# Decoder trunk layer: the first merge's token tiles in the places of three token combinations, and dilated queries turned on chip

## The chip, the cores and the metric

One core of a Trainium2 chip runs the whole kernel. The metric is device microseconds of one execution, as a median of several runs; lower is better. Everything is float32, and matmul operands are split into a high part and a low part (each a tile that the program calls fp32r), so that one product is three matmuls: high by high, high by low, low by high.

## The reference

One layer of a decoder trunk over 1024 tokens of width 1024, cut to what matters here:

```python
xn = _modulate(_rmsnorm(x, norm1), sh1, sc1)
z = xn @ w_in                       # au av bx bg q k v (768 each), 3 gates of 1024
out_a = _mixer_a(a_u, a_v, ...)     # chunked gMLP
out_b = _mixer_b(b_x, b_g, ...)     # RG-LRU recurrence
out_c = _mixer_c(c_q, c_k, c_v, rel_table)
gates = sigmoid(z_gate.reshape(bsz, s, 3, D_MODEL))
merged = gates[0]*(out_a @ p_a) + gates[1]*(out_b @ p_b) + gates[2]*(out_c @ p_c)
x = x + g1 * (merged @ w_out)
...
def _mixer_c(q, k, v, rel_table):   # 12 heads of 64
    for window, dil in ((128, 1), (512, 4), (2048, 16)):
        o, l = _dilated_attn(q * 64**-0.5, k, v, window, dil, rel_table)
    # the outputs weighted by softmax of the log-sums, then summed
```

## The kernel before, in words

**The projection stream.** `xn @ w_in` runs as units of seven steps (a Strassen-Winograd scheme): in each step twelve matmuls of 512 columns (line 295) multiply one combination of a weight pair's blocks (A11, A12, S1, S2, S3, A22, S4) by one combination of the tokens (B11, B21, T1, T2, T3, T4, B22). Each token combination lies split in eight tiles of a pool of its own, `xc1B11`, `xc1B21` and so on. So B11 is read in the first step of a unit only, B21 in the second, T1 in the third. After a step ACT or DVE moves a PSUM bank into the output tile `ot` (L161, L163, L165, L267, L269, L170, L172); of `ot` there are two buffers. A step S3 adds into the bank that the evacuation L165 of S2 reads, and S4 into the bank that L269 reads, which comes after L267. The units stand in a list (`Stream`), and its order is kept on all five engines; weights are prepared some steps ahead (L252, L254, L258). Its last nine units are three for queries, three for keys, and the gate units 18, 20 and 22. Gate units end with sigmoids (L677) and stores into `g_scr`.

**Queries and keys.** After a query or key unit `split_heads` makes from each half of `ot` the high part `h` (L924, ACT) and the low part in place (L927 or L929, DVE), and stores them to DRAM. Queries are stored twice, in token order and in an order in which a block of 128 tokens has its four residues modulo four in runs of 32; the second order is made by ACT (L933). `late`, side work that is fed in beside these units, forms modulation vectors from `w_ada` (POOL's DMAs, DVE, four small matmuls at each end).

**Attention and the first merges.** Once side work of the `hl` and `ad` pools has ended, a pool `hd` takes their place and head 0 is loaded (`load_head`, POOL's queue, and 16 small bias loads on SP). Then a second phase interleaves 12 heads with the merges of the branches, in an order written as planned times: head h starts at time h, and merge work (`filler`) is spread over F0 to F1. Only TensorE's order is fixed there; the other engines are ordered by the compiler's scheduler, which also lets work of this phase in among the last steps of the stream. `logits` forms seven banks for a head: four of dilation 1 (`cfg` 0) with 128 neighbouring columns of `qp` as weights, and three of dilation 4 (`cfg` 1: two with six matmuls, four of 128 and two of 256 columns, and one with four of 256) whose weights are every fourth column of `qn` and whose moving columns are every fourth of the keys. Two banks take turns. `merge` needs its branch's tokens split into tiles `oT` (lines 1117, 116, 117), the branch's weights (`p_a`, line 124, split by 116 and 117) and gates from `g_scr`. `oT` lies in pools `mrg0` and `mrg1`, which open when the stream's pools close, over the places of B11, B21 and T1. From SP's queue DMAs are issued in order; `raw` tiles have four buffers.

Of the kernel before, what the change touches and what calls it, by code (L numbers as in the profile page):

```python
# [20 lines left out]
P = 128  # L21
# [15 lines left out]
LEAD, DQ, TM, DP, DO = 0.55, 0.08, 1.05, 0.11, 0.18  # L37
FL, F0, F1 = -0.2, 0.1, 13.3
# [31 lines left out]
def trunk(ctx: ExitStack, tc: tile.TileContext, I: dict, out: bass.AP, dbg=None):  # L70
# [22 lines left out]
    def rows_scr(name, n):  # L93
# [3 lines left out]
    qk_scr = {n: [dram.tile(sh, F32, name=f"{n}{h}_scr") for h in range(NH)]  # L97
              for n, sh in (("q", [2, 2, HD, S]), ("k", [2, HD, S]))}
# [174 lines left out]
    def stream_ws(gb, tcomb, views, ot, post):  # L273
# [10 lines left out]
        for i, (wn, tn, bk) in enumerate(ORDER):  # L284
# [123 lines left out]
    xc = {n: x1.enter_context(tc.tile_pool(name=f"xc1{n}", bufs=1, side="right"))  # L408
          for n in ("B11", "B21", "T1", "B22", "T4", "T3")}
# [263 lines left out]
    def project(col, dst, f, j):  # L673

        def post(m0, m1):
            flat = [m.rearrange("p a b -> p (a b)") for m in (m0, m1)]
            res = [(1, lambda i=i: act.activation(flat[i], flat[i], f)) for i in (1, 0) if f]  # L677
            return res + [(2 if f else 1, lambda i=i: nc.scalar.dma_start(dst[j + i], flat[i])) for i in (1, 0)]
# [237 lines left out]
    def store_heads(name, ix, j, t):  # L916
        for i in range(2):
            nc.scalar.dma_start(qk_scr[name][2 * j + i][ix], t[HD * i:HD * i + HD, :])

    def split_heads(name, j, m, scale, hlp):  # L920

        mf = m.rearrange("p a b -> p (a b)")
        h = hlp().tile([P, S], F32R, tag="hl", bufs=3, name="hl")
        act.activation(h, mf, AF.Copy, scale=scale)  # L924
        yield
        if scale == 1.0:
            dve.tensor_tensor(mf.bitcast(F32R), mf, h.bitcast(F32), op=OP.subtract)  # L927
        else:
            dve.scalar_tensor_tensor(mf.bitcast(F32R), mf, scale, h.bitcast(F32), op0=OP.mult, op1=OP.subtract)  # L929
        for c, src in enumerate((h.bitcast(F32), mf)):  # L930
            if name == "q":
                dst = hlp().tile([P, S], F32, tag="hl", bufs=3, name="hlp")
                act.activation(dst.rearrange("p (t r i) -> p t r i", t=NT, r=4),  # L933
                               src.rearrange("p (t i r) -> p t r i", t=NT, r=4), AF.Copy)
                store_heads("q", (1, c), j, src)
                yield
                store_heads("q", (0, c), j, dst)
            else:
                yield
                store_heads("k", (c,), j, src)  # L940

    def project_heads(name, j, hlp):
        def post(m0, m1):
            def queue():
                for i, m in ((1, m1), (0, m0)):
                    side.append(split_heads(name, j + i, m, -0.125 if name == "q" else 1.0, hlp))

            return [(1, queue)]
# [3 lines left out]
    def late(ad):  # L952
# [15 lines left out]
        for i, (a, h, k) in enumerate(order):  # L968
# [7 lines left out]
            if k:  # L976
                yield
# [20 lines left out]
        for q in range(2):  # L998
            scale_cols(mod2, "norm2", q)

# [47 lines left out]
    gate_units(18, 20)  # L1048
# [8 lines left out]
    def load_head(h):  # L1057
        def tl():
            return heads["hd"].tile([P, 2, S], F32R, tag="qk", bufs=2, name="qk") if h % 2 == 0 else \
                wk.tile([P, 2, S], F32R, tag="ot", bufs=2, name="qk")  # L1060

        qq, kk = tl(), tl()
        nc.gpsimd.dma_start(qq, qk_scr["q"][h].rearrange("a c b s -> (c b) a s"))
        for i in range(2):
            nc.gpsimd.dma_start(kk[HD * i:HD * i + HD], qk_scr["k"][h].rearrange("c b s -> b c s"))
        qp, qn, kh, kl = qq[:, 0], qq[:, 1], kk[:, 0], kk[:, 1]
# [660 lines left out]
```

## Time and profile before

| | |
|---|---|
| median of 3 runs | 1984.4 us (1983.62 to 1989.04) |
| the profiled execution's own time | 1982.27 us |
| its span, first to last instruction | 1980.6 us |
| TensorE busy | 1874.4 us, 95% of the span |
| VectorE, ScalarE, GpSimd busy | 1287.9, 899.5 and 633.8 us |
| mean granted TensorE clock | 0.984 of full speed |

Rows below give microseconds from the span's start. PE is TensorE's matmuls, PEld its weight loads, DVE VectorE, ACT ScalarE, POOL GpSimd; a name with q behind it is that engine's issuing queue. A figure in brackets at a row's end is the idle time of the engine ahead of that row and who ended it. A timeline row with x6 merges six instructions, and its time reaches to the end of the last.

### The profile page before, as it was taken

The numbers are of one execution on the slowest core, as the hardware profiler recorded it, in microseconds if no ns is written. First come the engines' busy times: TensorE is split into PE (matmuls) and PEld (weight loads), VectorE is DVE, ScalarE is ACT, GpSimd is POOL, SyncE is SP. The second block draws the span as 40 slices with busy tenths as digits, with TensorE's granted clock in tenths as the row PEclk, the third lists the DMA queues.
The fourth block names the chain that finished last, engine by engine and source line by source line (L and its number), as shares of the span: only waits on it lengthen the run. The fifth ranks groups of instructions, "written<-read, shape, count | busy, mean of one in ns | idle before, by whom it ended". The sixth has DMA issues, their size and how long they took to land.

```text
span 1980.6 us, 26351 instructions
## 1 busy us (share of the span) xinstructions
PE 1874.4 (95%) x9119; PEld 1508.4 (76%) x9119; DVE 1287.9 (65%) x2259; ACT 899.5 (45%) x1644; POOL 633.8 (32%) x1067
## 2 busy tenths in 40 slices
PE   6899999999999899899899999999999999999996
PEld 5767898877767677677777777877787887877885
DVE  6766576666666675555555765569767666557786
ACT  5344556664335633534434533444433443344543
POOL 6310000003111111244555565456544444300002
PEclk9899999999999999899999999999999999999998
DMA  9232435435556888777677445413334333477674
GB/s 326 70 122 84 140 104 165 140 129 173 172 178 218 291 243 235 217 167 188 166 167 186 126 169 181 150 64 123 122 114 149 99 97 124 135 271 254 201 228 147
DMA packets 248118, 328.61 MB, mean 166 GB/s; under 512 B 16551, under 2 KB 167315, under 8 KB 247984
## 3 DMA queue, kind: packets, MB, share of 16 engines
q1 hardware_dynamic: 197664, 184.07, 31.4%
q10 hardware_dynamic: 33744, 87.18, 12.1%
q0 software_dynamic: 16576, 55.67, 10.1%
q8 instruction: 72, 1.18, 0.2%
q14 instruction: 62, 0.51, 0.1%
HBM read 238.64 MB, written 88.22 MB: 165 GB/s over the span
## 4 chain that ended last, share of the span: by engine, by line
PE 72%; DMA 9%; DVE 6%; issue 6%; POOL 3%; ACT 2%; SPq 1%; ACTq 0%; DVEq 0%; POOLq 0%
PE g L191 18%; PE g L295 18%; PE gp L1152 7%; PE g L334 6%; PE g L1615 6%; PE go L1407 4%; PE sl L1214 3%; DMA adaw<-in_w_ada_dram 2%; PE g L215 2%; PE tp L1258 1%; PE o L1287 1%; PE gp L1370 1%; PE m L788 1%; DMA res<-x_scr 1%; PE o L1290 1%
## 5 line engine op out<-in xcount | busy, mean ns | idle before, releaser
L295 PE MATMUL g<-xs,wh 128*128 128x512 f32 x1344 | 435.9, 405 | 31.1 <-ACT ot L165 21.7
L191 PE MATMUL g<-xs,wh 128*128 128x512 f32 x1176 | 367.6, 394 | 9.5 <-DVE up L168 2.7
L295 PEld LDWEIGHTS g<-xs,wh 128*128 128x128 f32 x1344 | 251.3, 190 | 107.8 <-ACT ot L165 32.1
L116 ACT ACTIVATE wh<-raw 128x512 fp32r<-128x512 f32 (+2 forms) x251 | 147.2, 601 | 274.2 <-issue 58.8
L191 PEld LDWEIGHTS g<-xs,wh 128*128 128x128 f32 x1176 | 220.3, 188 | 63.0 <-ACT xs L116 3.1
L295 PE MATMUL g<-xs,wl 128*128 128x512 f32 x672 | 267.9, 399 | 0.0
L191 PE MATMUL g<-xs,wl 128*128 128x512 f32 x588 | 230.4, 393 | 0.0
L117 DVE TENSOR_TENSOR wl<-raw,wh 128x512 fp32r<-128x512 f32 (+2 forms) x180 | 129.8, 727 | 84.2 <-ACT wh L116 84.0
L1152 PE MATMUL gp<-oT,wh 128*128 128x512 f32 x512 | 171.7, 415 | 4.4 <-ACT oT L116 1.9
L295 PEld LDWEIGHTS g<-xs,wl 128*128 128x128 f32 x672 | 127.8, 190 | 31.2
L117 POOL TENSOR_TENSOR wl<-st,wh 128x512 fp32r<-128x512 f32 x63 | 104.0, 1651 | 144.3 <-ACT wh L116 139.4
L117 POOL TENSOR_TENSOR wl<-raw,wh 128x512 fp32r<-128x512 f32 (+2 forms) x71 | 92.3, 1301 | 123.1 <-ACT wh L116 108.4
L254 ACT ACTIVATE wh<-st 128x512 fp32r<-128x512 f32 x120 | 75.2, 627 | 120.6 <-DVE st L252 120.4
L191 PEld LDWEIGHTS g<-xs,wl 128*128 128x128 f32 x588 | 110.5, 188 | 24.9
L334 PE MATMUL g<-wh,xs 128*128 128x256 f32 x672 | 124.8, 286 | 0.0
L116 ACT ACTIVATE wh<-st 128x512 fp32r<-128x512 f32 x95 | 59.3, 628 | 138.9 <-PE g L191 96.8
L1222 ACT ACTIVATE pm<-pm,stat 128x128 f32<-128x128 f32 (+1 forms) x192 | 89.0, 465 | 58.0 <-DVE stat L1219 57.9
L1152 PEld LDWEIGHTS gp<-oT,wh 128*128 128x128 f32 x512 | 89.8, 192 | 27.2 <-issue 7.7
L334 PEld LDWEIGHTS g<-wh,xs 128*128 128x128 f32 x672 | 103.7, 188 | 1.6 <-issue 1.0
L1615 PE MATMUL g<-wl,wh 128*128 128x512 f32 x264 | 103.5, 392 | 0.0
L1615 PE MATMUL g<-wh,wl 128*128 128x512 f32 x264 | 103.4, 392 | 0.0
L1152 PE MATMUL gp<-oT,wl 128*128 128x512 f32 x256 | 102.7, 401 | 0.0
(321 smaller groups left out, 3790.2 us busy)
## 6 DMA issues: line engine op xcount, KB each, us to landing
raw<-in_w_in_dram SPq DMA_DIRECT2D x66, 512.0 KB, 5.7
raw<-in_f_wdown_dram SPq DMA_DIRECT2D x77, 256.0 KB, 3.7
adaw<-in_w_ada_dram SPq DMA_DIRECT2D x48, 256.0 KB, 5.4
g_scr<-ot ACTq DMA_DIRECT2D x24, 512.0 KB, 5.2
adaw<-in_w_ada_dram POOLq DMA_DIRECT2D x48, 256.0 KB, 5.1
raw<-g_scr SPq DMA_DIRECT2D x24, 512.0 KB, 3.6
qk<-q_scr POOLq DMA_DIRECT2D x12, 1024.0 KB, 6.1
qk<-k_scr POOLq DMA_DIRECT2D x24, 512.0 KB, 9.6
```

Of the source, the lines that this page charges most:

```text
L116: act.activation(h, src, AF.Copy)
L117: l_eng.tensor_tensor(l, src, h.bitcast(F32), op=OP.subtract)
L191: pe.matmul(banks[bk], a[:, k, :], b, start=(fresh and j == 0), stop=(j == 11), skip_group_check=True)
L215: pe.matmul(banks[i, h], a[:, k, :], b, start=(fresh and j == 0), stop=(not fresh and j == 11), skip_group_check=True)
L254: act.activation(it["h"], bl[name], AF.Copy)
L295: pe.matmul(banks[bk], a[:, k, :], b, start=(fresh and j == 0), stop=(j == 11), skip_group_check=True)
L334: pe.matmul(banks[t2][bk][:, 256 * i:256 * i + 256], a[:, sl], b[:, k % 2, :], start=(fresh and i == 0 and j == 0), stop=(j == 11), skip_g ...
L1152: pe.matmul(pt, a_[:, k % g, :], b_, start=(j == 0), stop=(j == 3 * n - 1))
L1214: pe.matmul(sb[:, of:of + n], lq, kt[:, ks], start=(of == 0 and kt is kh), stop=(kt is kl), skip_group_check=True)
L1222: act.activation(pm[:, of:of + n], pm[:, of:of + n], AF.Exp, scale=-1.0, bias=stt[:, cfg, 0, idx:idx + 1], accum_out=stt[:, cfg, 1, idx:id ...
L1407: pe.matmul(pt, a_[:, sl], b_, start=(k == 0 and j == 0), stop=(k == KD - 1 and j == 2))
L1615: pe.matmul(bank, a_[:, sl], b_, start=(start and j == 0), stop=(j == 2), skip_group_check=True)
```

## The change

Three things. The tiles `oT` come from the pools of B11, B21 and T1 themselves, which now stay open for the merges, and the loads of branch a with the first gates and weights are written into the stream: first half of the tokens and gate 0 three steps from the end, second half and gate 1 two steps from it, the split of three tiles in the last step, the other nine behind it. The queries are stored once, high and low, in the four-residue order only; the copy is made by the split itself (ACT reads every fourth column), and the low part has a tile of its own, so that `ot` is not held by stores. For each head `turn_queries` makes from it on chip (two ACT copies of 512 columns) a tile `qd` in which the 128 queries of a residue, four tokens apart, lie side by side, so that the weights of the dilated logits are 128 neighbouring columns; keys are read as before. Also: both halves of a unit's output are finished each for itself (`post` takes one half), gate unit 20 moves behind the opening of `hd`, `late` yields six times in eight instead of seven, and heads are loaded 1.2 ahead instead of 0.55.

```diff
-LEAD, DQ, TM, DP, DO = 0.55, 0.08, 1.05, 0.11, 0.18
-FL, F0, F1 = -0.2, 0.1, 13.3
+LEAD, DQ, TM, DP, DO = 1.2, 0.08, 1.05, 0.11, 0.18
+F0, F1 = 0.1, 13.3
...
-                return later + (post(m0, m1) if wn == "S4" else [])
+                return later + (post(0, m0) if wn == "S4" else post(1, m1) if wn == "A22" else [])
...
+    mp_s = ctx.enter_context(ExitStack())
+    xc = {n: mp_s.enter_context(tc.tile_pool(name=f"xc1{n}", bufs=1, side="right")) for n in ("B11", "B21", "T1")}
...
+    def split_heads(name, j, m, hlp):
...
+        h, l = [hlp().tile([P, S], F32R, tag="hl", bufs=3, name="hl") for _ in range(2)]
+        if name == "q":
+            by4 = [t.rearrange("p (t r i) -> p t r i", t=NT, r=4) for t in (h, l)]
+            src = mf.rearrange("p (t i r) -> p t r i", t=NT, r=4)
+            act.activation(by4[0], src, AF.Copy, scale=-0.125)
+            yield
+            for r in range(4):
+                dve.scalar_tensor_tensor(by4[1][:, :, r, :], src[:, :, r, :], -0.125, by4[0][:, :, r, :].bitcast(F32),
+                                         op0=OP.mult, op1=OP.subtract)
...
-            if k:
+            if k % 4:
                 yield
...
+    def oT(h):
+        name = ("B11", "B21", "T1")[(12 * h + n_oT[h] % 12) // 8]
+        n_oT[h] += 1
+        return xc[name].tile([P, HALF], F32R, tag=name, bufs=8, name="oT")
...
-    gate_units(18, 20)
+    gate_units(18)
...
+    def turn_queries(qp):
+
+        qd = heads["hd"].tile([P, S], F32R, tag="qd", bufs=1, name="qd")
+        for j in range(0, S, HALF):
+            act.activation(qd[:, j:j + HALF].rearrange("p (r c i) -> p r c i", r=4, c=4),
+                           qp[:, j:j + HALF].bitcast(F32).rearrange("p (c r i) -> p r c i", r=4, c=4), AF.Copy)
+        return qd
...
-    gate_units(22)
+    gate_units(20, 22)
+    xa, first_a = {}, {}
...
+    for d, f in ((-3, lambda: xa.update(fetch_branch("a", 0, range(KW)))),
+                 (-3, lambda: first_a.update({0: fetch_merge("a", 0, 0)})),
+                 (-2, lambda: xa.update(fetch_branch("a", 1, range(KW)))),
+                 (-2, lambda: first_a.update({1: fetch_merge("a", 0, 1)})),
+                 (-1, lambda: split_some(0, (0, 1, 2)))):
+        marks.append((stream.n + d, f))
     stream.call(marks)
+    heads["qd"] = turn_queries(heads[0][0])
+    split_some(0, (3, 4, 5))
+    split_some(1, range(KW))
...
-                    lq = qn[:, 512 * j + r:512 * j + r + 509:4]
+                    lq = st_["qd"][:, P * idx:P * idx + P]
...
-        yield h - LEAD, load
+        yield max(h - LEAD, 0.3 * h), load
+        if h:
+            yield h - 0.3, turn_heads
```

On SP's queue, at the end of the stream, before the change: `raw` tiles (gates, and weights `p_a`) stand between the branch loads.

```order
L124 DMA raw<-g_scr 128x1024
L124 DMA raw<-in_p_a_dram 128x6x128
L1117 DMA oT<-oa_scr 128x512
L124 DMA raw<-g_scr 128x1024
L1117 DMA oT<-oa_scr 128x512
L124 DMA raw<-in_p_a_dram 128x6x128
L1117 DMA oT<-oa_scr 128x512 x3
L124 DMA raw<-g_scr 128x1024
L1117 DMA oT<-oa_scr 128x512 x6
L1172 DMA v_7105<-v_scr 128x8x128
```

And with it:

```order
L1098 DMA bt<-b_scr 32x256 x16
L1007 DMA oT<-oa_scr 128x512 x6
L124 DMA raw<-g_scr 128x1024
L124 DMA raw<-in_p_a_dram 128x6x128
L1007 DMA oT<-oa_scr 128x512 x6
L124 DMA raw<-g_scr 128x1024
L124 DMA raw<-in_p_a_dram 128x6x128
L124 DMA raw<-g_scr 128x1024
```

The bias loads have moved ahead of everything, each half of the branch comes in one run, and the first weights stand behind the first half.

On ACT, around the evacuations L165 and L267 of the stream's last unit, before (L677 are the last unit's sigmoids, L1222 the first head's exponentials):

```order
L678 DMA g_scr<-ot 128x1024 x2
L116 ACTIVATE wh<-raw 128x384 x4
L116 ACTIVATE oT<-oT 128x512
L165 ACTIVATE ot<-g 128x512
L116 ACTIVATE oT<-oT 128x512
L116 ACTIVATE wh<-raw 128x384
L116 ACTIVATE oT<-oT 128x512
L116 ACTIVATE wh<-raw 128x384
L267 ACTIVATE ot<-g 128x512
L1222 ACT_TABLE_LOAD
L1222 ACTIVATE pm,stat<-pm,stat 128x128
L1222 ACTIVATE pm,stat<-pm,stat 128x256 x3
```

And with it, from behind L267 on; ahead of these rows stand L165, one pair of weight splits (L116) and L267 (L678 are the sigmoids, L1256 the exponentials, L1105 the turned queries):

```order
L116 ACTIVATE oT<-oT 128x512 x3
L1256 ACT_TABLE_LOAD
L1256 ACTIVATE pm,stat<-pm,stat 128x128
L1256 ACTIVATE pm,stat<-pm,stat 128x256 x3
L678 ACT_TABLE_LOAD
L678 ACTIVATE ot<-ot 128x1024
L678 DMA g_scr<-ot 128x1024
L116 ACTIVATE wh<-raw 128x384 x2
L678 ACTIVATE ot<-ot 128x1024
L678 DMA g_scr<-ot 128x1024
L1105 ACTIVATE qd<-qp 128x512 x2
L116 ACTIVATE oT<-oT 128x512 x9
```

No split stands ahead of L165 any more, one pair of weights ahead of L267, and nine of the twelve token splits come behind both sigmoids and the turned queries.

On ACT in a query unit, before:

```order
L924 ACTIVATE hl<-ot 128x1024
L254 ACTIVATE wh<-raw 128x512
L933 ACTIVATE hlp<-hl 128x1024
L918 DMA q_scr<-hl 64x1024 x2
L254 ACTIVATE wh<-raw 128x512
L918 DMA q_scr<-hlp 64x1024 x2
L933 ACTIVATE hlp<-ot 128x1024
L918 DMA q_scr<-ot 64x1024 x2
L165 ACTIVATE ot<-g 128x512
```

And with it (L927 makes the high part, already in the four-residue order):

```order
L927 ACTIVATE hl<-ot 128x1024
L254 ACTIVATE wh<-raw 128x512
L918 DMA q_scr<-hl 64x1024 x2
L165 ACTIVATE ot<-g 128x512
L254 ACTIVATE wh<-st 128x512
L918 DMA q_scr<-hl 64x1024 x2
```

Both extra copies are gone from the place ahead of L165. On TensorE the matmuls are the same in number; the first eight of head 0's logits stood 36 matmuls ahead of the stream's end and now stand 120 ahead of it.

## Rows read from the trace of the kernel before

**Rows 1.** The page: its first line and TensorE's clock in 40 slices.
```profile
span 1980.6 us, 26351 instructions
PEclk9899999999999999899999999999999999999998
```

**Rows 2.** Windows: busy time and instructions of each engine, clock, DMA share and rate.
```profile
core 0: us, PE busy (x) PEld busy (x) DVE busy (x) ACT busy (x) POOL busy (x), PEclk, DMA share, GB/s
597.00:618.00 21.00, 20.31 (x86) 15.84 (x85) 12.96 (x22) 6.96 (x12) 3.75 (x7) 1.00 0.64 213
640.00:665.00 25.00, 21.91 (x87) 16.47 (x87) 15.96 (x24) 15.99 (x17) 3.30 (x7) 0.93 0.85 278
785.00:830.00 45.00, 33.78 (x131) 26.05 (x130) 19.11 (x55) 23.49 (x56) 11.08 (x38) 0.85 0.86 244
830.00:1176.00 346.00, 338.56 (x2032) 268.47 (x2031) 200.33 (x701) 150.17 (x484) 185.50 (x549) 0.99 0.65 159
```

**Rows 3.** Waits of TensorE from 785 to 830: total, times, longest.
```profile
PE g L295 <- DVE ot L269: 4.6, 1, 4.6
PE g L295 <- ACT ot L165: 2.2, 1, 2.2
```

**Rows 4.** Timeline at the end of the stream, ACT and TensorE.
```profile
786.48 0.94 ACT L116 ACTIVATE wh<-raw 128x384 fp32r<-128x384 f32 x2 [6.04 <-DMA raw<-in_p_a_dram]
...
787.84 0.57 ACT L165 ACTIVATE ot<-g 128x512 f32<-128x512 f32 x1
...
796.29 0.63 ACT L116 ACTIVATE oT<-oT 128x512 fp32r<-128x512 f32 x1 [2.88 <-DMA oT<-oa_scr]
...
797.24 0.58 ACT L267 ACTIVATE ot<-g 128x512 f32<-128x512 f32 x1
...
797.84 1.28 ACT L1222 ACT_TABLE_LOAD   x1
...
798.99 1.22 PE L295 MATMUL g<-xs,wh 128*128 128x512 f32 x2 [4.64 <-DVE ot L269]
...
799.54 0.49 ACT L1222 ACTIVATE pm<-pm,stat 128x256 f32<-128x256 f32 x1
```

**Rows 5.** Timeline in the query units, ACT and TensorE.
```profile
651.28 2.03 ACT L933 ACTIVATE hlp<-ot 128x1024 f32<-128x1024 f32 x1 [0.73 <-DVE adaa L975]
...
653.22 0.58 ACT L165 ACTIVATE ot<-g 128x512 f32<-128x512 f32 x1
...
653.85 1.22 PE L295 MATMUL g<-xs,wh 128*128 128x512 f32 x2 [3.08 <-ACT ot L165]
...
679.16 0.73 PE L295 MATMUL g<-xs,wh 128*128 128x512 f32 x2 [2.81 <-ACT ot L165]
```

**Rows 6.** ACT's copies of 128x1024: plain, and with every fourth column (ns min/median/max).
```profile
L924 ACT ACTIVATE hl<-ot x12: 1051/1056/1063, 621.6 to 745.7; 128x1024 fp32r<-128x1024 f32 x12
...
L933 ACT ACTIVATE hlp<-ot x6: 2028/2068/2096, 626.4 to 688.2; 128x1024 f32<-128x1024 f32 x6
```

**Rows 7.** Logits of one head, loads and matmuls: dilation 1 from 886.5, dilation 4 from 894.5.
```profile
L1214 PEld LDWEIGHTS sl<-qk x8: 187/189/192, 886.6 to 887.9; 128*128 128x128 f32 x8
...
L1214 PEld LDWEIGHTS sl<-qk x6: 315/330/333, 894.7 to 895.8; 128*128 128x128 f32 x6
...
886.85 0.62 PE L1214 MATMUL sl<-qk 128*128 128x128 f32 x4
887.31 0.49 PE L1258 MATMUL tp<-ident,pm 128*128 128x128 f32 x3
887.55 0.72 PE L1214 MATMUL sl<-qk 128*128 128x256 f32 x4
888.11 0.62 PE L1152 MATMUL gp<-oT,wh 128*128 128x512 f32 x2
...
894.92 1.55 PE L1214 MATMUL sl<-qk 128*128 128x128 f32 x6
896.40 0.66 PE L1287 MATMUL o<-st,v 128*64 128x128 f32 x8
...
901.07 1.32 PE L1214 MATMUL sl<-qk 128*128 128x256 f32 x4
902.21 0.62 PE L1258 MATMUL tp<-ident,pm 128*128 128x128 f32 x4
```

More of the change, by code (lines that the diff above doesn't have):

```diff
@@ L96, in trunk @@
     z_scr = {n: rows_scr(n, KW) for n in ("au", "bx", "bg")}
-    qk_scr = {n: [dram.tile(sh, F32, name=f"{n}{h}_scr") for h in range(NH)]
-              for n, sh in (("q", [2, 2, HD, S]), ("k", [2, HD, S]))}
+    qk_scr = {n: [dram.tile([2, HD, S], F32, name=f"{n}{h}_scr") for h in range(NH)]
+              for n in "qk"}
     g_scr = rows_scr("g", 3 * KD)
@@ L673, in project, with post @@
     def project(col, dst, f, j):
[L675 to L678, printed above, removed]
+        def post(i, m):
+            flat = m.rearrange("p a b -> p (a b)")
+            return [(1, lambda: act.activation(flat, flat, f)), (2, lambda: nc.scalar.dma_start(dst[j + i], flat))]
         return stream_ws(gb1, tcomb, pair_views(col, j), ot2, post)
@@ L942, in project_heads @@
-    def project_heads(name, j, hlp):
[L943 to L948, printed above, removed]
+        h, l = [hlp().tile([P, S], F32R, tag="hl", bufs=3, name="hl") for _ in range(2)]
[7 more added lines that the diff above has]
+                                         op0=OP.mult, op1=OP.subtract)
+        else:
+            act.activation(h, mf, AF.Copy)
+            yield
+            dve.tensor_tensor(l, mf, h.bitcast(F32), op=OP.subtract)
@@ L999, in late, with fetch_branch, split_branch, load_branch @@
             scale_cols(mod2, "norm2", q)
+    n_oT = [0, 0]
+    def oT(h):
+        name = ("B11", "B21", "T1")[(12 * h + n_oT[h] % 12) // 8]
+        n_oT[h] += 1
+        return xc[name].tile([P, HALF], F32R, tag=name, bufs=8, name="oT")
+    def fetch_branch(b, h, ks):
+        res = {}
+        for k in ks:
+            hh, ll = res[k, h] = oT(h), oT(h)
+            nc.sync.dma_start(ll.bitcast(F32), o_scr[b][k][:, HALF * h:HALF * h + HALF])
+        return res
+    def split_branch(b, tiles):
+        for (k, _), (hh, ll) in tiles.items():
+            split_to(hh, ll, ll.bitcast(F32), dve if b == "a" or k % 2 == 0 else pool)
+    def load_branch(b, h, ks):
+        res = fetch_branch(b, h, ks)
+        split_branch(b, res)
+        return res
+    def fetch_merge(b, zi, co, k0=0, k1=KW):
+        return (raw_tile(g_scr[zi * KD + co], [S]),
+                raw_tile(kview(I["p_" + b], co * P, P, k0 * P, k1 * P), [k1 - k0, P]))
     sched = ctx.enter_context(ExitStack())
@@ L1057, in load_head @@
     def load_head(h):
[L1058 to L1063, printed above, removed]
+        if h % 2 == 0:
+            qp = heads["hd"].tile([P, S], F32R, tag="qp", bufs=1, name="qp")
+            kk = heads["hd"].tile([P, 2, S], F32R, tag="qk", bufs=1, name="qk")
+        else:
+            qp, kk = [wk.tile([P, 2, S], F32R, tag="ot", bufs=2, name="qk") for _ in range(2)]
+            qp = qp[:, 0]
+        nc.gpsimd.dma_start(qp, qk_scr["q"][h].rearrange("c b s -> (c b) s"))
         for i in range(2):
             nc.gpsimd.dma_start(kk[HD * i:HD * i + HD], qk_scr["k"][h].rearrange("c b s -> b c s"))
-        qp, qn, kh, kl = qq[:, 0], qq[:, 1], kk[:, 0], kk[:, 1]
+        kh, kl = kk[:, 0], kk[:, 1]
         bt = heads["hd"].tile([P, 2, 256], F32, tag="bt", bufs=2, name="bt")
@@ L1326, in filler @@
     def filler():
-        xa, xb_, xc_ = {}, {}, {}
-        for h in range(2):
-            xa.update(load_branch("a", h, range(KW)))
-        yield
-        yield from merge("a", 0, emit_first, xa, lambda h: xb_.update(load_branch("b", h, range(KW))))
+        xb_, xc_ = {}, {}
+        yield from merge("a", 0, emit_first, xa, lambda h: xb_.update(load_branch("b", h, range(KW))), fetched=first_a)
         yield from merge("b", 1, emit_more, xb_, lambda h: xc_.update(load_branch("c", h, range(CSPLIT))))
```

58 lines of the change are left out of this document (17 added, 41 removed).

## The prediction, made before the changed kernel ran

> **What bounds the kernel now.** I read the page first: TensorE is granted nearly full speed everywhere, except in the first slice, one near the middle and the last [rows 1]. The slice near the middle is where the projection stream ends. Then the windows by stage [rows 2]. In a quiet unit (597 to 618) TensorE works 20.31 of 21 us; 86 matmuls are recorded, 0.236 us each, so a step of twelve takes 2.83 us. Three stretches differ. From 640 to 665 (query units) it idles 3.1 us and its clock is 0.93. From 785 to 830 (end of the stream, first merge, head 0) it works 33.78 of 45 us at a mean clock of 0.85. From 830 to 1176 (heads and merges) it works 338.56 of 346 us: there only fewer or shorter TensorE instructions help. No other engine comes near: DVE has 200.33 us, POOL 185.50, ACT 150.17 in that stretch.
>
> Next the waits of the end of the stream [rows 3]: TensorE stands still for 4.6 us until DVE's L269 and 2.2 until ACT's L165, both evacuations of the last unit; smaller waits make up the rest of the 11.2 us. The timeline says why [rows 4]. ACT's queue holds splits for the first merge ahead of the evacuations: it waits 6.04 us for the weights `p_a` with L165 behind, and 2.88 us for a token tile with L267 behind. L267 then starts at 797.24, L269 follows, and step S4 at 798.99. The weights and tokens come late because SP issues them in turn with `raw` tiles that wait for a buffer.
>
> In the query units the same evacuation L165 stands behind a 2.03 us copy with stride four, and TensorE waits 3.08 and 2.81 us for it [rows 5].
>
> **The end of the stream.** What it costs before: 11.2 us of idling, and the clock. At 0.85 over 45 us at most 6.75 us are lost to it, 5.1 if I count busy time alone (0.15 of 33.78). Together 16.3. In the changed order no split stands ahead of L165, so its wait falls to that of other units (about 0.7: the bank has to be moved before S3 may add to it). L267 has only one pair of weights ahead. I take the second wait as gone, and then add up what stands between L267 and the fourth token split, because TensorE needs that one for its ninth matmul of the first merge: L267 0.58, three token splits at 0.6, two table loads at 1.28, four exponentials at 0.49, two sigmoids of 128x1024 at 1.06 (priced as the plain copy), a pair of weights 0.94, two turned-query copies at 1.03 (half of 2.07 each), the split 0.6 [rows 4, 6]. That is 0.6 + 1.8 + 2.6 + 2.0 + 2.1 + 0.9 + 2.1 + 0.6 = 12.7 us after S3 ends. TensorE by then has done A22 and S4 (5.7), nine merge matmuls (2.1) and four logits (0.6): 8.4. So a **new wait of about 4.3 us** stands in front of the ninth merge matmul, with everything else of TensorE queued behind it, and a wait of 4.64 us was followed by slow matmuls (1.22 us for two, as against 0.73 elsewhere [rows 4, 5]); I add 2.5 us for that. With 0.7 for L165 and 1 us in case the first weights land late (they are now issued behind half the tokens, and the DMA engines are 0.86 busy [rows 2]): 8.5 us remain of 16.3. Gain 8. Bounds: 13 if the new wait doesn't cost, 2 if the weights are late by the old 6.04 us again.
>
> **The heads.** The weights of the dilated logits change from every fourth column to neighbouring columns. One load of the strided kind takes 330 ns, of the plain kind 189 [rows 7]. What matters is from start to start: a bank with four 128-column and two 256-column matmuls runs from 894.92 to 896.40, 1.48 us, and one with four of 256 from 901.07 to 902.21, 1.14. With plain weights and plain keys four of 256 took 0.56 (887.55 to 888.11), and two of 128 with two of 256 took 0.46, so 0.14 and 0.09 each. The keys remain strided, and no row has plain weights with strided keys. Bounds: if the keys cost nothing, the banks fall to 0.64, 0.64 and 0.56, which saves 2.26 us a head. If a 256-column matmul is held at 0.247 us (1.48 / 6) by its keys alone, and a 128-column one at half of that, the six take 0.99 and only the two mixed banks gain, 0.5 each: 1.0 a head. A mixed bank spends 0.247 per matmul though most have half the columns of the other bank, whose four take 0.285; so its short ones are surely held by the weights, the long ones perhaps by both. I take 1.2 a head, near the lower end because a moving column with stride four has no reason to be cheaper than a weight column with it. Eleven heads (head 0 lies in the stretch above): 13 us, bounds 11 and 25. If other engines swallow half, 5.5.
>
> For this ACT turns queries, 2.07 us a head [rows 6], 25 us in all, beside 150.17 busy of 346: its queue has room, and the copies stand 0.3 of a head ahead (a head takes 346 / 12, some 28 us, so 8 us) of the first logits that need them. Behind them in the queue are exponentials and the moves of turned probabilities, which TensorE needs later. DMA bytes fall (queries once instead of twice); nothing waits for them, I count nothing.
>
> The Trainium skill ("SBUF — State Buffer", the cacheline note in Door 1) says that SBUF is read in lines of 16 bytes and that every access to a new line pays. The trace agrees for ACT: 2068 ns against 1056 for the same elements [rows 6]. By that rule a stride of four float32 values pays in the keys as in the weights, the lower of my bounds.
>
> **The query and key units.** Per query tile ACT spent 1.06 + 2 x 2.07 us; now one strided copy, 2.07 [rows 6]. The copies ahead of L165 are gone and `ot` is free without its stores. DVE's low part becomes four strided pieces; DVE has room (15.96 of 25 us [rows 2]). The waits of 3.08 and 2.81 fall to 0.7 each (4.5), and the clock gives back at most 0.07 of 25 us (1.75 [rows 2]). Gain 5, bounds 6.2 and 0 (three `hl` tiles now serve four uses a unit and hold their places until stored; if ACT waits for them, L165 stands behind that).
>
> **Costed at nothing.** Finishing halves apart (three more table loads on ACT by the changed order, 3.8 us, hidden by TensorE's steps); `late` in fewer steps; head 0 loaded a unit earlier. This last has a price if its cover goes: head 0's first logits stand 120 matmuls from the end, 28 us (0.236 each); if the load is late, the whole stream waits behind them.
>
> **The sum.** 1982.3 us, the profiled execution's own time (1.7 more than its span, 2.1 less than the median of 1984.4), less 8, 13 and 5: **1956 us**.
>
> **Rivals.**
> - *Keys are free, weights were all.* 25 us in the heads instead of 13: 1944. For it: 330 ns loads in every dilated bank. Against: the keys have the same stride. The Trainium skill ("TensorE: Matmul & The Clock Gate", Back-to-back issue gap) says that spacing is set by load and matmul together, pipelined; no run here shows which of the two holds the long ones.
> - *The heads give little, or the new wait takes the end of the stream.* 5.5 in the heads, 4 at the end, 3 in the units: 1970. For it: DVE and POOL are over half busy in the heads, and a logits bank is free only when DVE has read it; a shorter bank then waits. Against: TensorE waits for little there (7.4 us in 346, [rows 2]).
> - *No change.* ACT's 25 us of copies and the 4.3 us wait eat the 26 us. That needs 2 us lost in each head; 1982.
> - *Slower.* One mechanism: TensorE waits in each head for ACT's two turned copies (2.07 us), with slow matmuls behind each wait as after the 3.08 us wait (1.22 for 0.73, some 1.5 us). 11 x 3.6 = 40 us against 26: 1996. It decides from 2.4 us a head. Against: 8 us between copy and use.
>
> **How the numbers follow.** Chances: the forecast (1948 to 1965) 0.5; free keys 0.15; little 0.21; no change 0.07; slower 0.07. Range: the ends of the bounds give 1982.3 - 13 - 25 - 6 = 1938 and 1982.3 - 2 - 5.5 = 1975; leaving out the last two cases, and the corners where all bounds meet, 1942 to 1972. A measurement here tells a change from none at about 0.3%, 6 us: faster (below 1978) 0.86, within 0.07, slower 0.07.
>
> **What would show it.** Right: no TensorE wait for L269 over 1 us at the end of the stream, one wait of 3 to 6 us for a token split (`oT`) in the first merge; L1248's loads at 189 ns throughout, mixed banks near 1.0 us from start to start, the four of 256 near 1.0 still; no waits over 1 us for L165 in the query units. Wrong: mixed banks at 0.64 (free keys); waits for `stat` or ACT's moves in each head; TensorE waiting for head 0's queries or bias ahead of the last unit.

## The result, and the profile after

The changed kernel takes 1964.6 us in the median (1961.2 to 1967.9), the kernel before 1984.9 beside it: ratio 0.9893, interval 0.9867 to 0.992. The first profiled execution of the changed kernel ran at a clock of 0.653 and took 2606.8 us, so the profile below is of a second profiled execution, the first experiment's: 1965.5 us with a span of 1963.4.

The page, its first line and the clock in slices:

```profile
span 1963.4 us, 26382 instructions
PEclk9899999999999999899999999999999999999998
```

The slice near the middle still falls below 9. To see where the time went, cut both executions at the same TensorE rows of the timeline: first row of the first query unit, of gate unit 18, of the last unit, the stream's last row, the 73rd merge matmul (the end of merge's first four banks), the last merge matmul.

| us | before | after | |
|---|---|---|---|
| up to the first query unit | 596.7 | 597.7 | +1.0 |
| six query and key units | 135.2 | 132.9 | -2.3 |
| gate units 18 and 20 | 42.1 | 42.6 | +0.5 |
| last unit | 30.1 | 20.6 | -9.5 |
| stream's end to the 73rd merge matmul | 34.9 | 39.9 | +5.0 |
| heads and merges, to the last merge matmul | 337.1 | 322.4 | -14.7 |
| the rest | 804.5 | 807.2 | +2.7 |

The last three stages ahead of the rest as windows, before (three rows) and after (last unit, up to the 73rd matmul, heads); columns as in [rows 2]:

```profile
774.00:804.10 30.10, 23.27 (x93) 18.13 (x91) 11.86 (x23) 15.21 (x29) 4.20 (x4) 0.89 0.80 242
804.10:839.00 34.90, 30.22 (x136) 24.24 (x136) 20.65 (x74) 17.07 (x51) 12.02 (x48) 0.90 0.82 202
839.00:1176.10 337.10, 329.94 (x1982) 261.04 (x1982) 192.10 (x666) 145.75 (x469) 181.92 (x535) 0.99 0.65 161
```

```profile
773.30:793.90 20.60, 19.91 (x85) 15.52 (x83) 8.83 (x20) 10.39 (x21) 1.59 (x2) 1.00 0.95 330
793.90:833.80 39.90, 29.34 (x137) 23.60 (x137) 22.75 (x77) 23.99 (x65) 16.15 (x51) 0.87 0.75 179
833.80:1156.20 322.40, 317.52 (x1981) 245.29 (x1980) 193.68 (x666) 155.27 (x488) 181.10 (x534) 0.99 0.61 152
```

In the last unit TensorE idles 0.7 us instead of 6.8, at full clock. The stretch behind it became worse: TensorE idles 10.6 us of 39.9 where it idled 4.7 of 34.9, and its clock is 0.87 for 0.90. In the heads, busy time fell by 12.4 us and idling by 2.3.

What TensorE waited for from 780 to 834, after (total, times, longest):

```profile
PE o L1321 <- POOL wl L117: 6.4, 1, 6.4
PE gp L1181 <- ACT oT L116: 3.0, 1, 3.0
PE gp L1181 <- DVE ot L172: 0.9, 1, 0.9
PE g L295 <- ACT ot L165: 0.7, 1, 0.7
```

The 4.6 us for L269 of [rows 3] are gone and L165 is at 0.7, as forecast. The forecast wait for a token split is there (3.0). The longest wait, 6.4 us, was in no forecast. The timeline shows both, put in order of time across the engines:

```profile
799.03 1.15 ACT L1105 ACTIVATE qd<-qp 128x512 fp32r<-128x512 f32 x2 [0.46 <-ACT ot L678]
...
800.75 1.52 PE L1181 MATMUL gp<-oT,wh 128*128 128x512 f32 x2 [3.02 <-ACT oT L116]
...
811.53 10.28 SPq L1098 DMA_DIRECT2D bt<-b_scr  x8
...
822.08 0.39 SPq L124 DMA_DIRECT2D raw<-in_p_a_dram  x1
...
825.53 0.94 ACT L116 ACTIVATE wh<-raw 128x384 fp32r<-128x384 f32 x2 [9.24 <-DMA raw<-in_p_a_dram]
...
826.09 0.56 DVE L117 TENSOR_TENSOR wl<-raw,wh 128x384 fp32r<-128x384 f32 x1 [4.75 <-ACT wh L116]
...
827.77 0.55 DVE L1297 COPY st<-tp 128x384 f32<-128x384 f32 x1
...
828.42 1.12 PE L1321 MATMUL o<-st,v 128*64 128x128 f32 x6 [6.43 <-POOL wl L117]
```

Read it upward. TensorE's first outputs need the turned probabilities `st`, which DVE copies at 827.77. Ahead of this copy in DVE's queue stands the low part of the fourth merge weights, which waits 4.75 us for ACT's high part, which waits 9.24 us for the load; SP issued the load at 822.08, behind eight bias loads that took it 10.28 us. (The row of waits names POOL's half of the same low part; it is DVE's that stands in the way.) The Trainium skill ("TensorE: Matmul & The Clock Gate", Architectural detail) says that VectorE and ScalarE take instructions strictly first in, first out. The trace agrees: the transposes that the copy reads had ended by 822.0, and 4.75 us of idle DVE stood ahead of it.

In the query units:

```profile
631.32 2.20 DVE L930 SCALAR_TENSOR_TENSOR hl<-ot,hl 128x256 fp32r<-128x256 f32 x4 [4.41 <-DMA q_scr<-hl]
...
638.27 0.69 DVE L269 TENSOR_TENSOR ot<-g,ot 128x512 f32<-128x512 f32 x1
...
639.01 0.73 PE L295 MATMUL g<-xs,wh 128*128 128x512 f32 x2 [2.44 <-DVE ot L269]
```

ACT no longer holds L165 up as in [rows 5], but DVE's low part waits for an `hl` tile that a store still reads, and DVE's L269, late behind it, holds TensorE up.

The dilated logits of one head, answering to [rows 7]:

```profile
887.84 1.10 PE L1248 MATMUL sl<-qk,qd 128*128 128x128 f32 x6
888.87 0.66 PE L1321 MATMUL o<-st,v 128*64 128x128 f32 x8
...
892.97 1.18 PE L1248 MATMUL sl<-qk,qd 128*128 128x256 f32 x4
893.97 0.62 PE L1292 MATMUL tp<-ident,pm 128*128 128x128 f32 x4
```

From start to start a mixed bank takes 1.03 us and the bank of four 256-column matmuls 1.00, where 1.48 and 1.14 were shown before.

### The profile page after: what moved, and what is told of

Read it like the earlier page. It is cut to its first block, busy times and chain, and to the rows that moved or that the text cites. A ratio compares the mean times of both kernels' runs of the same rounds, so it can differ in the third digit from the quotient of the medians.

```text
span 2604.6 us, 26382 instructions
## 1 busy us (share of the span) xinstructions
PE 2553.7 (98%) x9119; PEld 1689.1 (65%) x9119; DVE 1292.2 (50%) x2277; ACT 901.5 (35%) x1659; POOL 620.9 (24%) x1067
## 4 chain that ended last, share of the span: by engine, by line
PE 96%; issue 1%; DVE 1%; POOL 1%; ACT 1%; DMA 0%; POOLq 0%; DVEq 0%; SPq 0%
PE g L295 25%; PE g L191 22%; PE g L1647 10%; PE gp L1181 10%; PE g L334 6%; PE go L1439 5%; PE g L215 5%; PE sl L1248 3%; PE tp L1292 2%; PE o L1321 1%; PE o L1324 1%; PE gp L1402 1%; PE m L788 1%; PE m L884 1%; ACT ot L165 0%
## 5 line engine op out<-in xcount | busy, mean ns | idle before, releaser
L295 PE MATMUL g<-xs,wh 128*128 128x512 f32 x1344 | 568.3, 512 | 16.1 <-ACT ot L165 14.3
L191 PE MATMUL g<-xs,wh 128*128 128x512 f32 x1176 | 490.2, 507 | 0.0
L295 PEld LDWEIGHTS g<-xs,wh 128*128 128x128 f32 x1344 | 277.0, 209 | 189.1 <-issue 58.2
L295 PE MATMUL g<-xs,wl 128*128 128x512 f32 x672 | 341.7, 508 | 0.0
L191 PEld LDWEIGHTS g<-xs,wh 128*128 128x128 f32 x1176 | 243.3, 207 | 141.7 <-issue 47.4
L116 ACT ACTIVATE wh<-raw 128x512 fp32r<-128x512 f32 (+2 forms) x251 | 146.8, 600 | 478.7 <-PE g L191 143.4
L191 PE MATMUL g<-xs,wl 128*128 128x512 f32 x588 | 297.7, 507 | 0.0
L1181 PE MATMUL gp<-oT,wh 128*128 128x512 f32 x512 | 219.1, 518 | 1.0 <-DVE ot L172 0.9
L334 PE MATMUL g<-wh,xs 128*128 128x256 f32 x672 | 167.9, 349 | 0.0
L334 PEld LDWEIGHTS g<-wh,xs 128*128 128x128 f32 x672 | 139.3, 249 | 3.0 <-issue 1.9
L116 ACT ACTIVATE wh<-st 128x512 fp32r<-128x512 f32 x95 | 59.7, 629 | 231.8 <-PE g L191 211.1
L1647 PE MATMUL g<-wh,wl 128*128 128x512 f32 x264 | 133.8, 507 | 0.0
L1647 PE MATMUL g<-wl,wh 128*128 128x512 f32 x264 | 133.7, 507 | 0.0
L1181 PE MATMUL gp<-oT,wl 128*128 128x512 f32 x256 | 130.1, 508 | 0.0
L1647 PE MATMUL g<-wh 128*128 128x512 f32 x264 | 122.7, 507 | 0.0
```

The source lines that it names most:

```text
L116: act.activation(h, src, AF.Copy)
L191: pe.matmul(banks[bk], a[:, k, :], b, start=(fresh and j == 0), stop=(j == 11), skip_group_check=True)
L295: pe.matmul(banks[bk], a[:, k, :], b, start=(fresh and j == 0), stop=(j == 11), skip_group_check=True)
L334: pe.matmul(banks[t2][bk][:, 256 * i:256 * i + 256], a[:, sl], b[:, k % 2, :], start=(fresh and i == 0 and j == 0), stop=(j == 11), skip_g ...
L1181: pe.matmul(pt, a_[:, k % g, :], b_, start=(j == 0), stop=(j == 3 * n - 1))
L1647: pe.matmul(bank, a_[:, sl], b_, start=(start and j == 0), stop=(j == 2), skip_group_check=True)
```

## The experiments

Twelve runs. Each ratio is to the kernel before, run beside it, with its 95% interval; from one experiment to another it is ratios that are compared, and stages are read from one profiled execution each.

**The changed kernel again** (no edit).

> The changed kernel once more, for a profile with TensorE at full clock. It should take 1961 to 1968 us. The prediction's three terms are read from it: 8 us at the end of the stream, 13 in the heads, 5 in the query and key units. My theory before looking: since the total fell by 20 and not 26, the heads gave the lower bound or less (11 us), and the end of the stream 4 to 6, because the new wait for the fourth token split is there. Rival: the heads gave 13 or more and the query units nothing.

1965.4 us, ratio 0.989 (0.9869 to 0.9911). It is the base below. The theory of the heads fell (14.7 us, not 11 or less); that of the end of the stream held (4.5).

**Keys plain.**

```diff
-                    ks = slice(r, r + 4 * n - 3, 4)
+                    ks = slice(0, n)
```

> Keys of the dilated logits are read as neighbouring columns instead of every fourth (other keys, so other numbers come out; the instructions are the same). If strided keys hold the long matmuls of the dilated banks, the mixed bank falls to about 0.64 us and the bank of four 256-column matmuls to 0.56, and the time falls by a further 8 to 13 us. If the keys are free (the rival that would have given 1944), nothing changes, and the mixed bank is at 0.64 already.

1960.4 us, ratio 0.9854 (0.983 to 0.9878). Heads 316.9 us, 5.5 less than after the change and short of the 8 to 13 expected. The banks, in the timeline:

```profile
890.28 0.84 PE L1248 MATMUL sl<-qk,qd 128*128 128x128 f32 x6
891.05 0.66 PE L1321 MATMUL o<-st,v 128*64 128x128 f32 x8
...
894.89 0.74 PE L1248 MATMUL sl<-qk,qd 128*128 128x256 f32 x4
895.47 0.60 PE L1292 MATMUL tp<-ident,pm 128*128 128x128 f32 x4
```

0.77 and 0.58 us, against 1.03 and 1.00: the keys' stride costs what the change left in these banks. Over 22 mixed banks and 11 others that is 22 x 0.26 + 11 x 0.42 = 10.3 us, of which 5.5 reach the stage: shorter banks meet other waits, and TensorE idles 8.6 us there where it idled 4.9.

**Weights strided again, out of the turned tile.**

```diff
-                    lq = st_["qd"][:, P * idx:P * idx + P]
+                    lq = st_["qd"][:, HALF * j + r:HALF * j + r + 509:4]
```

> The turned tile is made but the dilated logits read every fourth column of it as weights, as the kernel before did (other queries, so other numbers come out). This undoes the heads' part alone and leaves ACT's turned copies. By the prediction's lower bound it costs 11 us against the changed kernel, by its value 13, and loads are at 330 ns again. If the heads gave little (the third rival), it costs 0 to 5 us.

1977.9 us, ratio 0.9951 (0.9933 to 0.9969); heads 335.2 us. The weight loads of one group of the lines (ns min/median/max) are those of before again:

```profile
L1248 PEld LDWEIGHTS sl<-qk,qd x165: 307/330/337, 839.8 to 1132.7; 128*128 128x128 f32 x165
```

So 335.2 - 322.4 = 12.8 us of the heads' 14.7 come from the weights alone.

**All first splits ahead of the turned queries.**

```diff
-                 (-1, lambda: split_some(0, (0, 1, 2)))):
+                 (-1, lambda: split_some(0, range(KW)))):
...
-    heads["qd"] = turn_queries(heads[0][0])
-    split_some(0, (3, 4, 5))
     split_some(1, range(KW))
+    heads["qd"] = turn_queries(heads[0][0])
```

> All six token splits of the first half stand in the stream's last step, and the second half's splits ahead of the turned queries. By the prediction the wait of about 4 us ahead of the first merge's ninth matmul then goes, with the slow matmuls behind it: 4 to 7 us less than the changed kernel. If that wait is not there, or another takes its place (the first dilated logits for the turned queries, S4 for L269), 0 to 2 us.

1963.3 us, ratio 0.9874 (0.9851 to 0.9896), which doesn't part it from the base. The profile shows that the 3.0 us wait is gone (2.3 for L172 and 2.1 for ACT's turned queries stand in its place), and the 6.4 us wait too, though the same weights are as late. In DVE's timeline the two instructions have changed places:

```profile
821.95 0.55 DVE L1296 COPY st<-tp 128x384 f32<-128x384 f32 x1
...
824.66 0.56 DVE L117 TENSOR_TENSOR wl<-raw,wh 128x384 fp32r<-128x384 f32 x1 [1.02 <-ACT wh L116]
```

So what late weights cost TensorE hangs on what the scheduler put behind their split: here it is no longer this copy.

**Branch loaded late.** The marks with the early loads are taken out, and the filler loads the branch itself again, in a first step at -0.2.

```diff
-    for d, f in ((-3, lambda: xa.update(fetch_branch("a", 0, range(KW)))),
...
-    split_some(0, (3, 4, 5))
-    split_some(1, range(KW))
...
+        for h in range(2):
+            xa.update(load_branch("a", h, range(KW)))
+        yield
+        yield from merge("a", 0, emit_first, xa, lambda h: xb_.update(load_branch("b", h, range(KW))))
```

> The changed kernel, with the loads and splits of the first branch and of the first two merges' weights put back behind the stream's end, as in the kernel before; their tiles stay where the change put them. Theory (early loading is worth the 8 us that the prediction gave the end of the stream): about 8 us slower than the changed kernel, 1973 us, with TensorE waiting over 10 us in all for the branch tiles between the last unit and the ninth merge matmul. Rival (most of it is given back anyway by a wait of 6 us some 25 us later, which the changed kernel has and this one has not): 2 to 4 us slower, 1968 us, and no wait of 6 us of the first outputs.

1962.5 us, ratio 0.9885 (0.9865 to 0.9906): not slower at all, where theory and rival both had a loss. Without them the last unit takes 23.7 us and the next stretch 34.6, together 58.3 against the base's 60.5 and 65.0 before. (These stages are of an execution of 1955.7 us, 6.7 below the run's median and its quickest.)

**The old places as well.** The former run, and the pools of the kernel before for the branch.

```diff
-        return xc[name].tile([P, HALF], F32R, tag=name, bufs=8, name="oT")
+        return mrg[h].tile([P, HALF], F32R, tag="oT", bufs=2 * KW, name="oT")
...
+    mp_s = ctx.enter_context(ExitStack())
+    mrg = [mp_s.enter_context(tc.tile_pool(name=f"mrg{h}", bufs=1, side="right")) for h in range(2)]
```

> The run with the branch loaded late, and its tiles put back as well where the kernel before had them, in pools of their own that open when the token combinations are closed; heads and query units stay changed. Theory (the places are what the end of the stream gains by, since the loads can start while the last unit runs; the explicit early loads add nothing): 8 to 11 us slower than with late loads alone, 1972 us, with branch loads still issued after the last unit's end and waits of several us for the branch and for L269 back in the last unit. Rival (the gain there comes from head 0 loaded a unit earlier and the smoother evacuation): within 3 us of late loads alone, 1963 us.

1953.7 us (1952.9 to 1956.7), ratio 0.9835 (0.9819 to 0.9852): the fastest version, clear of the changed kernel's interval. Undoing what the title names first, the places, with the early loads, gains some 11 us (0.0055 of 1985; the two intervals leave 6 to 16). The theory fell, and its rival was too timid. The windows of the same three stages:

```profile
772.70:794.50 21.80, 20.01 (x85) 15.52 (x83) 13.53 (x27) 15.17 (x31) 2.60 (x3) 1.00 0.89 302
794.50:827.80 33.30, 26.35 (x137) 22.17 (x137) 18.07 (x71) 18.24 (x51) 13.55 (x50) 0.98 0.78 179
827.80:1145.80 318.00, 315.76 (x1982) 243.96 (x1982) 194.23 (x666) 156.34 (x491) 181.75 (x534) 1.00 0.61 155
```

And TensorE's waits from 760 to 835, with one row of ACT's twelve splits of the branch:

```profile
PE sl L1236 <- ACT st L1283: 4.9, 1, 4.9
PE gp L1169 <- DVE ot L172: 2.0, 1, 2.0
PE g L295 <- ACT ot L165: 1.8, 1, 1.8
...
L116 ACT ACTIVATE oT<-oT x12: 614/618/634, 782.9 to 797.3; 128x512 fp32r<-128x512 f32 x12
```

The last unit is quick (21.8 us) without new places and without early loads, no wait for a token split is left, and the clock behind the stream is 0.98 where the base has 0.87. The fourth weights are late here too, at 4.9 us.

What then mended the last unit? SP's queue, before (four rows) and in this run (three rows):

```profile
767.78 10.21 SPq L1075 DMA_DIRECT2D bt<-b_scr  x11
...
778.62 0.39 SPq L124 DMA_DIRECT2D raw<-in_p_a_dram  x1
...
788.51 0.38 SPq L124 DMA_DIRECT2D raw<-in_p_a_dram  x1
...
798.53 0.32 SPq L124 DMA_DIRECT2D raw<-g_scr  x1
```

```profile
748.67 11.27 SPq L1095 DMA_DIRECT2D bt<-b_scr  x14
...
775.49 0.39 SPq L124 DMA_DIRECT2D raw<-in_p_a_dram  x1
...
778.53 7.20 SPq L1004 DMA_DIRECT2D oT<-oa_scr  x12
```

In the kernel before, the bias loads of heads 0 and 1 (eight each) held SP up to 778. Behind them came the second weights, and then branch loads cut up by `raw` tiles that waited for a buffer, among them the third weights at 788.51 and the fourth gate at 798.53; the last branch load started at 812.5. With the heads opened one unit earlier, fourteen of the sixteen bias loads are through at 759.9, 18 us sooner. Little of that reaches the loads behind: the second weights wait for a `raw` buffer and go out 3.1 us earlier, the first branch load 1.2 us earlier. The larger difference is that no `raw` tile stands between the twelve branch loads any more. They follow each other from 778.5, inside the last unit and not behind it as the theory had them, and ACT has seven of them split by the time it comes to L267. What is left of the change at this place is the earlier heads, the outputs finished half by half, gate unit 20 in a new place and `late` in fewer steps. These weren't run apart, so which of them put the loads into this order isn't shown.

**Bias loads later.**

```diff
+        def bias():
+            st_["in"] = st_["in"][:3] + (load_bias(h),)
...
+            yield h - 0.3, bias
             yield h - 0.3, turn_heads
```

> The changed kernel, with the bias loads of heads 1 to 11 moved from 1.2 heads to 0.3 heads ahead of their head, so that three of the eight that stood ahead of the fourth merge weights on SP's queue stand behind them. Theory (the wait of 6.4 us of the first outputs comes from the last of these bias loads, which waits for a queue slot held by a gate load): the weights are issued some 5 us earlier, the wait falls under 2 us, 1960 us. Rival (the weights are late because the transfers are slow there, whatever stands ahead of them on the queue): the wait stays at 4 us or more, 1965 us.

1968.1 us, ratio 0.9909 (0.989 to 0.9929): no gain. The weights' load, ACT's split and the outputs:

```profile
813.56 0.39 SPq L124 DMA_DIRECT2D raw<-in_p_a_dram  x1
...
822.53 0.94 ACT L116 ACTIVATE wh<-raw 128x384 fp32r<-128x384 f32 x2 [6.53 <-DMA raw<-in_p_a_dram]
...
825.87 0.33 PE L1327 MATMUL o<-st,v 128*64 128x128 f32 x2 [3.89 <-issue]
```

Issued 8.5 us earlier, the weights take 9.0 us to reach ACT where the base's took 3.5, and TensorE still waits 3.9 us. The place on the queue was a part of it; in the base the DMA share is above 1 from 805 to 820, so crowded transfers are the likely rest, which no run shows apart. The rival was nearer.

**High parts stored first.**

```diff
             act.activation(by4[0], src, AF.Copy, scale=-0.125)
+            store_heads(name, 0, j, h.bitcast(F32))
             yield
```

(the same for keys, and the call behind the low part is dropped)

> The changed kernel, with the stores of the high parts in the query and key units issued right behind ScalarE's copy instead of behind VectorE's low part. Theory (VectorE waits for a tile whose store is late, and its addition and TensorE behind it): the waits of the low part for a store fall from 16.6 us in all to under 9, TensorE's waits for L269 in the query units from 3.8 us to under 2, 1 to 3 us faster, 1963 us. Rival (the stores take so long that 1.3 us matter little, or VectorE's four slow pieces themselves make it late): within 1 us, 1965 us.

1961.2 us, ratio 0.9872 (0.9852 to 0.9891); the intervals overlap with the base. One wait of DVE (from 610 to 790) and one of TensorE (from 610 to 760):

```profile
DVE hl L931 <- DMA q_scr<-hl: 2.4, 1, 2.4
...
PE g L295 <- DVE ot L269: 1.4, 3, 0.8
```

The low part's waits fall from 16.6 us to 2.4, TensorE's for L269 from 2.6 to 1.4 (the 3.8 of the expectation counts one ahead of these units), and the query and key units from 132.9 us to 130.7. Part of DVE's waiting moved: for the weight blocks of the side work it waits 12.4 us instead of 4.0. The theory holds for the mechanism; its size is 2 us.

**Four tiles.** `hl` gets four buffers, `adaw` one instead of three, and a weight block of the side work is fetched only behind the use of the one before.

```diff
-        h, l = [hlp().tile([P, S], F32R, tag="hl", bufs=3, name="hl") for _ in range(2)]
+        h, l = [hlp().tile([P, S], F32R, tag="hl", bufs=4, name="hl") for _ in range(2)]
...
-                raws[i] = ad.tile([P, HALF], F32, tag="adaw", bufs=3, name="adaw")
+                raws[i] = ad.tile([P, HALF], F32, tag="adaw", bufs=1, name="adaw")
```

> The changed kernel, with four tiles for the high and low parts of queries and keys instead of three, paid for by one buffer instead of three for the weight blocks of the side work (which is loaded one block ahead). Theory (three tiles for four uses a unit are what the query units lack): no wait of the low part for a store over 1 us, no TensorE wait for L269 over 1 us in the query units, 2 to 4 us faster, 1962 us. Rival (VectorE's four pieces of 0.6 us and ScalarE's 2.1 us copy are what is late): TensorE's waits as before, 1965 us. If VectorE waits for the one buffer of the side work instead: the same or up to 3 us slower.

2048.0 us, ratio 1.0317 (1.0296 to 1.0338). Nothing follows for `hl`: the price swallowed the test. One wait of DVE and two of TensorE, from 590 to 900:

```profile
DVE adaa L967 <- DMA adaw<-in_w_ada_dram: 106.6, 42, 6.9
```

```profile
PE m L988 <- DVE adaa L967: 37.0, 4, 9.9
PE g L295 <- DVE ot L269: 24.0, 7, 7.5
```

With one buffer DVE waits 42 times for a weight block of the side work, and the evacuations stand behind it. The expectation's 3 us for this case was too low by far.

**Plain query split.** High and low parts are written in the order read, one DVE instruction of 1.2 us for four; other queries reach the heads.

```diff
-            act.activation(by4[0], src, AF.Copy, scale=-0.125)
+            act.activation(h, mf, AF.Copy, scale=-0.125)
...
+            dve.scalar_tensor_tensor(l, mf, -0.125, h.bitcast(F32), op0=OP.mult, op1=OP.subtract)
```

> The changed kernel, with the query split writing its high and low parts in the order it reads them (one VectorE instruction of 1.2 us for four of 2.2 us in all, and a ScalarE copy of 1.1 us for 2.1 us), so that the queries reach the heads in another order and the output is of other queries. Theory (three tiles for four uses a unit set the query units, through stores of 8 us): the low part still waits for a store, first query unit still over 23 us, time within 1 us of the changed kernel, 1964 us. Rival (the slow access of every fourth number is what makes VectorE late): first two query units at 22 us or less, 2 to 4 us faster, 1961 us.

1958.9 us, ratio 0.9854 (0.9838 to 0.9871). Query and key units 130.1 us, 2.8 less than the base. The low part still waits 19.2 us in all for stores, as the theory had it, yet TensorE waits 0.9 at the longest for L269, and the gain is the rival's. So both the late tile and the slow pieces (ACT's copy is plain here too) make L269 late, and to mend either is enough. The 6.4 us wait is gone here as well, without an edit near it.

**Both orders.** The edits of "all first splits" and "high parts stored first" together.

> The changed kernel with two orders changed: all six splits of the first half in the stream's last unit with the rest ahead of the turned queries, and the stores of the high parts ahead of VectorE's low part. Theory (both gains stand apart: some 4 us at the first merge, where VectorE's copy of the first turned probabilities then stands ahead of the late weights' low part, and some 2 us in the query units): 1958 us, 5 to 7 us faster than the changed kernel, no wait over 3 us between the stream's end and the first outputs. Rival (the program's order on VectorE falls out differently again, and the late weights of the fourth merge block it): 1961 to 1965 us, with a wait of 4 us or more there.

1961.9 us, ratio 0.9874 (0.9853 to 0.9894). Not the sum: query and key units take 129.9 us, but this time TensorE's wait sits at another place:

```profile
PE sl L1248 <- ACT pm L1256: 3.3, 1, 3.3
PE gp L1181 <- DVE ot L172: 2.3, 1, 2.3
PE sl L1248 <- ACT qd L1106: 2.1, 1, 2.1
```

By DVE's timeline it is the late weights again: their low part, with 4.02 us of idling ahead of it at 824.41, now stands ahead of DVE's reads of the logits. The rival was right in its time and its mechanism, not in its 4 us: the order fell out anew here too.

**Heads loaded late.**

```diff
-LEAD, DQ, TM, DP, DO = 1.2, 0.08, 1.05, 0.11, 0.18
+LEAD, DQ, TM, DP, DO = 0.55, 0.08, 1.05, 0.11, 0.18
```

> The changed kernel, with the loads of each head 0.55 heads ahead as in the kernel before, and not 1.2; the queries are still turned 0.3 heads ahead. Theory (a load lands in 7.6 us, a quarter of a head is 6.7 us, so ScalarE would wait some 1 to 2 us for the queries it is to turn, in each head, which TensorE mostly doesn't see): 0 to 4 us slower than the changed kernel, 1967 us. Rival (ScalarE's wait holds the turned probabilities behind it, and TensorE waits in each head): 10 us or more slower, over 1975 us. If the early loads are what crowds the transfers at the first merge: the wait of 6 us there is gone and the time is 4 us better instead, 1960 us.

1967.8 us, ratio 0.991 (0.9888 to 0.9931), heads 323.1 us: as the theory had it, the lead of 1.2 is worth little. The wait of the first outputs is there (7.0 us), so the early loads don't cause it.

## Why the prediction was right, and where it was not

The time lies inside the range and 9 us above the point. The sum was 26 us. The medians show 20.3, the two profiles 17.2 (1980.6 to 1963.4), since the first is of an execution 2.6 us under the median beside it and the second of one 0.9 over. Below, terms are held against the profiles. Two misreadings did no harm: the low first slice of [rows 1] is the second, and it is the tenth merge matmul that needs the fourth token split.

**The heads: right.** Forecast 13, measured 14.7, of which 12.8 by the weights alone (335.2 against 322.4; the two ratios give 12). Mixed banks forecast 0.99, measured 1.03; the four of 256 "near 1.0", measured 1.00. The keys pay for their stride, as the lower bound had it; the rival with free keys is out, and even plain keys gave 0.77 for a mixed bank, not the 0.64 of the upper bound. By the Trainium skill ("SBUF — State Buffer", the cacheline note in Door 1) each access that crosses to a new 16-byte line pays a penalty. The trace agrees for a moving operand too: four of 256 columns take 1.00 us strided, 0.58 plain.

**The turned copies: mis-sized, without harm.** They were priced at 2.07 us a head as stride-four reads. They read runs of 32 numbers, and two take 1.15 us at 799.03, no more than plain copies of 128x512 (0.62 each). The new wait was 3.0 us and not 4.3, though the chain ahead of it was nearly as added up: 12.3 us from L267's start at 788.47 to TensorE's at 800.75, for 12.7. The rest is that TensorE came later itself, held up 0.9 us by L172. In the heads TensorE's list of waits has no row for them: the slower rival found nothing.

**The end of the stream: half right in size, wrong in cause.** Forecast 8, measured 9.5 - 5.0 = 4.5. "In the changed order no split stands ahead of L165", and the L269 wait gone, held. The step that failed is "8.5 us remain of 16.3": the sum stopped at the wait for the fourth token split, and 28 us later stood the 6.4 us wait for turned probabilities behind late weights, in no term and no rival. It and the 3.0 us wait left slow matmuls: the 137 recorded ones of the stretch take 29.34 us of TensorE, in the old places 26.35. The second failure is of cause. I gave this gain to the new order with its early loads; without them and without the new places this part gains 9.9 us (55.1 against 65.0), more than with them. What frees the last unit is then to be sought in what is left, items that stood under "costed at nothing" (head 0 loaded a unit earlier, halves finished apart, fewer steps of `late`) or weren't in the sum (gate unit 20). So that 4.5 us came out here, inside the bounds of 2 and 13, is partly luck. The upper bound, too, was added up short: with the new wait free, its own terms leave 16.3 - 0.7 - 1 = 14.6.

**The query and key units: half the size.** Forecast 5, measured 2.3. L165 came down as forecast (from 8.6 us in all to 3.4), but the waits for L269 grew from 0.8 to 2.6, and from 640 to 665 the granted clock stayed at 0.93. The named risk, three `hl` tiles, came true, on DVE and not on ACT: "DVE has room" was read from a busy share, but DVE stood idle 4.41 us at one low part with its other work queued behind. Earlier stores or quicker pieces each give back 2 to 3 us.

**Beyond the sum.** The stages behind the heads took 2.7 us more. Nothing there is changed; in the runs above they lie between 802.5 and 807.8 us, on both sides of the 804.5 before, so I take it for scatter.

**Open.** In the heads the old places save another 4.4 us. One wait of TensorE makes up most: 3.7 us at 938, where DVE reads logits late beside the splits of branch b. A wait of 3.5 to 4.3 us of that kind is there in all eleven profiles with the new places, and not with the old ones. Why the places order DVE differently wasn't settled. The profile with late loads alone is of an execution 6.7 us below its median, so the stages show only 2.9 of the 8.8 us between that run and the old places. And which of the remaining items mended the last unit wasn't run apart.

## What to carry to other kernels

A change of several parts should be undone part by part even when it wins: here the part that the title names first costs, with the early loads, some 11 us of a gain that the others make. When a sum follows a wait that is removed, go on to the next transfer on the same queue, and ask what stands behind its consumer on each in-order engine; a busy share doesn't answer that. Turn a strided operand by an engine that can read it in longer runs (32 numbers here), and count the operand that stays strided at its full price.

## What the runs showed of the hardware

Eight bias loads of 32 KB took SP 10.28 us to issue, and its list of waits puts 5.6 us of it down to a gate load issued just ahead:

```profile
SPq L1098 <- DMA raw<-g_scr: 5.6, 1, 5.6
```

Five of the eight went out in 2.25 us, and the last, which started at 821.50, is the one that waited. By that list, then, a DMA that needs nothing from another was held back by it, and everything behind it on the queue as well. With the last three moved behind the weights (bias loads later), the weights went out 8.5 us earlier.

Four DVE pieces of 128x256 that read every fourth number take 2.20 us in all, where the same instruction in one piece of 128x1024, reading in order (plain query split), takes 1.22. The runs don't part the stride from the number of pieces.
